# TensorE's order written by hand in the SSD stage of a two-layer hybrid decoder trunk

## The chip, the cores and the metric

The program runs on one core of a Trainium2 chip. It is measured in microseconds of device time; the time of a kernel is the median of its runs.

## The reference

A prompt of 256 tokens and 8 sample sequences of 4 tokens each pass through the same two layers. The kernel holds all 288 tokens as the columns of one tile (NT = 288). A layer is a half-step FFN, a mixer with two branches, and a second half-step FFN:

```python
x = x + 0.5 * swiglu(rmsnorm(x, norm_ffn1[l]), w_ffn1_gu[l], w_ffn1_down[l])
m, g_s, s_s, c_s = mixer(rmsnorm(x, norm_mix[l]), ...)
x = x + m
x = x + 0.5 * swiglu(rmsnorm(x, norm_ffn2[l]), w_ffn2_gu[l], w_ffn2_down[l])
```

```python
q, k, v, g, a_lr, z, xbc, dt_raw, gate_a, gate_b = jnp.split(u @ w_in, offs, axis=-1)
...
o_gla = rmsnorm(o_gla, gla_norm)
o_gla = o_gla * silu(g)
xbc_c = silu(causal_dwconv(xbc, conv0, conv_w, conv_b))
xs, Bm, Cm = jnp.split(xbc_c, ...)
y, ssm_new = ssd_chunked(xs, dt, A, Bm, Cm, ssm0)
y = rmsnorm((y + d_skip * xs) * silu(z), ssm_norm)
m = sigmoid(gate_a) * (o_gla @ w_proj_gla) + sigmoid(gate_b) * (y @ w_proj_ssm)
return m @ w_out, gla_new, ssm_new, conv_new
```

GLA is a chunked linear attention with a matrix state for each of 8 sequences and 4 heads. SSD is a chunked scan over 32 heads of width 64, in 4 groups that share B and C, with a 64 x 128 state for each of 8 sequences and 32 heads. The new states of both are outputs. Everything is float32.

## The kernel before, in words

**Projections.** Almost all of the work is the product of a weight matrix with the 288 token columns. A float32 weight block of 128 output columns is loaded as 128 x 8 x 128 and split by `split` into a high part (ACT, a copy, tile wh) and the rest (DVE or POOL, a subtraction, tile wl); the activations are split in the same way (xh, xl). A block is then 24 matmuls of 288 columns into one PSUM tile psg, of which there are three. `mm3` writes them: for each of 8 slices wh with xh and wh with xl (L177 and L178), then wl with xh for all 8 (L180). In this document a projection is one such matmul of 288 columns. `blocks` (L182) makes a sequence of such blocks.

**Small products.** Everything else on TensorE goes to PSUM tiles pst, of which there are four: transposes (`tr`, L142) and the products of the scans.

**Who sets the order.** The kernel is written in a tile framework whose scheduler orders each engine's instructions, TensorE's among them. The code says which blocks are interleaved with which stage: `gla` and `ssd` are generators, and at each `yield n` the loop `run` (L510) lets `F` emit n fill blocks. `F` (L503) is the sequence of the z, g, gate_gla and gate_ssm blocks with the GLA's output projection between them. Each `yield` of `F` is one whole block or, in `gated` and `project` (L550 to L564), a block and a projection.

**The end of GLA (L830 to L847).** The sums of squares of four heads are made by TensorE with a matrix of ones, two products for each head (L835, 8 in all), in four row groups of one PSUM tile. ACT takes the root (L837), DVE the reciprocal (L838), ACT and DVE split it in two rows of rp (L840, L841). At `yield 1` (L842) a fill block is emitted. Then four products of 2 rows (L845) spread rp over 128 partitions, and DVE scales o8 with it.

**The SSD stage (`ssd`).** It works on 16 pairs of heads, j = 0 to 15; an iteration is one j. Two j make a state pair hg, four j make a group g.
- `stage_bc(g)` projects the group's B and C blocks and runs the causal convolution (`conv`, L854) on each: ACT copies the block to a buffer, POOL adds the old columns, ACT and DVE sum four taps and apply SiLU. `stage_group(g)` transposes B, makes the scores C x B (three products, L933 to L935) and masks them. `stage_mask(g)` makes bm, eight copies of B with all but one sequence's rows zero (128 rows x 8 x 128, L952), in one buffer.
- `stage_x(j)` projects the block of xs and convolves it; `stage_m(j)` transposes it (three `tr`), scales it twice on DVE (xg at L1025, xd at L1028) and makes the decay mask m.
- `stage_load(j)` loads the states of 2 heads and 8 sequences into two tiles st (L962) of eight buffers, so those of four j. `stage_h(hg, i)` transposes four 128 x 128 states (L142) and copies them to sh; `stage_h2(hg, 3)` reads all of the pair's states with C (8 products, L985) and scales the result to yos (L990).
- `stage_y(j)` decays the states (8 POOL instructions of 128 columns, L1046), makes the scan's four products of m and xg (L1052, L1054), the sample's product (L1055) and the prompt's new state (L1057, L1058). DVE, POOL and ACT make y, the gated yf, its split yh and yr, and its squares. Then two products of 512 columns (L1076) make the state update, xpk x bm over 128 rows; DVE adds it to the states (L1078), and SP's queue stores them (L1080).

In iteration j come the load for j+3, transposes of the next pair, the projection of xs for j+2, state reads, `stage_m(j+1)`, a fill block, a transpose, `stage_y(j)` and one more fill block (two at every fourth j). After the last iteration `proj` (L519) emits the fill blocks that are left and the SSD's output projection.

## Time and profile before

| | us |
|---|---|
| median of 3 runs | 1853.45 |
| the runs | 1853.57, 1853.45, 1852.42 |
| profiled execution, its own time | 1856.72 |
| profiled execution, span of the trace | 1854.1 |

| engine | busy, share of the span | instructions |
|---|---|---|
| PE (matmul) | 98% | 13712 |
| DVE | 67% | 2074 |
| ACT | 56% | 1866 |
| POOL | 20% | 553 |

The trace is of one profiled execution; the time of that execution is a little longer than its span, by what lies around it. PE is TensorE's matmuls, PEld its weight loads, which lie beside them. The ends of matmuls are modelled, so the idle time of PE is known less well than the starts. PEclk is the clock that TensorE was granted, 1.00 being 2.4 GHz and 0.50 being 1.2 GHz; over the whole span it was 0.997. The first layer's SSD stage lies at about 375 to 645 us of the span, the second layer's at about 1290 to 1560 us.

### The profile page before, as it was taken

To read this page: it belongs to the slowest core of one execution; us is meant where nothing else is said; L and a number is where in the kernel's file an instruction comes from. 1 tells how busy PE (TensorE), PEld (TensorE's weight loads), DVE (VectorE), ACT (ScalarE), POOL (GpSimd) and SP (SyncE) were. 2 spreads that over 40 slices of the span, in tenths; PEclk is the share of its full clock that TensorE was granted. 3 is DMA by queue.
4 is the path that set the end of the run, shared out by engine and by line. 5 is a ranking of instruction groups with operands and counts; after the bars stand their busy time and mean duration, and the time that the engine had idled before them with its cause. 6 is when DMAs were issued, how large, how long until landed. Compare 5 with 4: busy or idle time off the path is not lost. (4 is left out here: it accounts for less than half of the span.)

```text
span 1854.1 us, 35076 instructions
## 1 busy us (share of the span) xinstructions
PE 1815.0 (98%) x13712; PEld 1745.5 (94%) x13712; DVE 1237.8 (67%) x2074; ACT 1038.3 (56%) x1866; POOL 377.6 (20%) x553
## 2 busy tenths in 40 slices
PE   8999999999999999999999999999999999999997
PEld 8999999888989899999999999998899888999997
DVE  6555577688877767555565556776887777665554
ACT  6444466567766646444454445665776675454443
POOL 1000000057667500000000000000777663000000
PEclk9999999999999999999999999999999999999999
DMA  7555654876778565555555555568587775655552
GB/s 214 166 164 158 165 153 127 262 193 180 212 194 223 166 169 173 165 166 162 172 167 161 161 164 158 144 183 251 153 225 199 199 206 151 172 165 165 162 162 89
DMA packets 613114, 325.43 MB, mean 176 GB/s; under 512 B 17090, under 2 KB 607986, under 8 KB 612948
## 3 DMA queue, kind: packets, MB, share of 16 engines
q1 hardware_dynamic: 612900, 323.07, 61.0%
q8 instruction: 107, 1.75, 0.4%
q14 instruction: 59, 0.48, 0.1%
q10 hardware_dynamic: 48, 0.13, 0.0%
HBM read 292.93 MB, written 30.22 MB: 174 GB/s over the span
## 5 line engine op out<-in xcount | busy, mean ns | idle before, releaser
L158 ACT ACTIVATE wh<-wr 128x1024 fp32r<-128x1024 f32 (+1 forms) x498 | 517.7, 1042 | 479.2 <-PE psg L178 384.6
L177 PE MATMUL psg<-xh,wh 128*128 128x288 f32 x2704 | 740.0, 300 | 2.8 <-ACT t L867 2.2
L178 PE MATMUL psg<-xl,wh 128*128 128x288 f32 x2704 | 734.5, 297 | 0.1
L164 DVE TENSOR_TENSOR wl<-wr,wh 128x1024 fp32r<-128x1024 f32 (+1 forms) x496 | 596.9, 1206 | 151.7 <-ACT wh L158 147.0
L177 PEld LDWEIGHTS psg<-xh,wh 128*128 128x128 f32 x2704 | 508.0, 188 | 9.7 <-issue 6.2
L178 PEld LDWEIGHTS psg<-xl,wh 128*128 128x128 f32 x2704 | 508.1, 188 | 3.3 <-issue 0.9
L180 PE MATMUL psg<-xh,wl 128*128 128x288 f32 x2704 | 416.1, 296 | 0.0
L180 PEld LDWEIGHTS psg<-xh,wl 128*128 128x128 f32 x2704 | 378.3, 188 | 2.0 <-issue 0.9
L1046 POOL TENSOR_SCALAR st<-st,decs 128x128 f32<-128x128 f32 x256 | 228.7, 907 | 18.7 <-PE pst L142 18.6
L177 PE MATMUL psg<-hh,wh 128*128 128x288 f32 x704 | 189.8, 296 | 0.0
L178 PE MATMUL psg<-hl,wh 128*128 128x288 f32 x704 | 189.5, 295 | 0.0
L372 POOL MEMSET cbuf<- 128x3 f32 x4 | 0.3, 108 | 654.4 <-DVE t L324 654.4
L178 PEld LDWEIGHTS psg<-hl,wh 128*128 128x128 f32 x704 | 132.7, 188 | 0.0
L177 PEld LDWEIGHTS psg<-hh,wh 128*128 128x128 f32 x704 | 132.2, 188 | 0.1
L304 DVE TENSOR_TENSOR t<-t,psg 128x288 f32<-128x288 f32 x88 | 40.0, 454 | 135.2 <-ACT wh L158 123.1
L180 PE MATMUL psg<-hh,wl 128*128 128x288 f32 x704 | 109.2, 295 | 0.0
L301 DVE TENSOR_TENSOR t<-psg,rr 128x288 f32<-128x288 f32 x88 | 40.3, 457 | 90.5 <-PE psg L180 90.5
L180 PEld LDWEIGHTS psg<-hh,wl 128*128 128x128 f32 x704 | 99.0, 188 | 0.0
L865 DVE SCALAR_TENSOR_TENSOR cacc<-cbuf,cw,cacc 128x312 f32<-128x312 f32 x144 | 78.1, 542 | 11.1 <-ACT cacc L863 10.7
L177 PE MATMUL psg<-yh,wh 128*128 128x288 f32 x256 | 70.2, 300 | 0.0
L178 PE MATMUL psg<-yb,wh 128*128 128x288 f32 x256 | 69.4, 296 | 0.7 <-DVE yb L1070 0.7
L177 PE MATMUL psg<-oh,wh 128*128 128x288 f32 x256 | 69.7, 299 | 0.0
(315 smaller groups left out, 2287.9 us busy)
## 6 DMA issues: line engine op xcount, KB each, us to landing
wr<-in_w_ffn_gu_dram SPq DMA_DIRECT2D x176, 512.0 KB
wr<-in_w_in_dram SPq DMA_DIRECT2D x160, 512.0 KB
wr<-in_w_ffn_down_dram SPq DMA_DIRECT2D x64, 448.0 KB
wr<-in_w_ffn_down_dram SPq DMA_DIRECT2D x32, 512.0 KB
st<-in_state_ssm_dram SPq DMA_DIRECT2D x64, 256.0 KB
out_dram<-st SPq DMA_DIRECT2D x64, 256.0 KB
wr<-in_w_proj_ssm_dram SPq DMA_DIRECT2D x32, 512.0 KB
gst<-in_state_gla_dram SPq DMA_DIRECT2D x32, 256.0 KB
```

The lines of the kernel that those rows point to most:

```text
L158: A.activation(out=h, in_=raw, func=AF.Copy)
L164: V.tensor_tensor(out=lo, in0=raw, in1=h, op=ALU.subtract)
L177: T.matmul(out, lhsT=h[:, k], rhs=xh[k], start=start and k == 0, stop=False)
L178: T.matmul(out, lhsT=h[:, k], rhs=xl[k], start=False, stop=False)
L180: T.matmul(out, lhsT=lo[:, k], rhs=xh[k], start=False, stop=stop and k == n - 1)
L301: V.tensor_tensor(out=t, in0=pg, in1=r, op=ALU.mult)
L304: V.tensor_tensor(out=h, in0=t, in1=pu, op=ALU.mult)
L372: G.memset(cbufs[i][:, 0:3], 0.0)
L865: V.scalar_tensor_tensor(out=acc, in0=buf[:, i:i + NCV], scalar=w[i], in1=acc, op0=ALU.mult, op1=ALU.add)
L1046: G.tensor_scalar(out=sts[hf][:, r], in0=sts[hf][:, r], scalar1=decs[:, n:n + 1], scalar2=None, op0=ALU.mult)
```

## The change

TensorE's order in the SSD stage is no longer the scheduler's. A flag `in_order` is set from the start of the stage's loop to its end, and while it is set every matmul and transpose is passed to `keep_in_program_order`, so that TensorE runs them as they are written. Other engines are still ordered by the scheduler.

- A block of 24 projections is now emitted in thirds of 8 (`mm3s`, `thirds`): a generator stops after the slices 0 to 3 and 4 to 7 of wh, and after the eight of wl. `D(n)` deals n thirds, first from `jobs` (the queue of convolution blocks that the stage has asked for), then from `F`. Calls of `D` stand between the small products of an iteration.
- The group products of the next group come at j%4 == 2, with a third between the transposes and the scores. The masks are made with them.
- `bm` has four copies instead of eight (seq4 for seq8), in two buffers instead of one. The first half of the rows of xpk holds sequences 0 to 3, the second half 4 to 7, so that the update is two products of 512 columns over 64 rows each (rows 0 to 63 and 64 to 127). The two state tiles of a j now hold sequences 0 to 3 and 4 to 7 instead of even and odd ones, and `stage_h` and `state_view` follow.
- The 16 decays of a state pair are emitted together right behind the pair's last transposes (`stage_decay`), instead of 8 in each `stage_y`.
- At j == 13 the first halves of the output projection's blocks 0 and 1 are put into `jobs` (`begin`); each holds its psg tile until `proj` completes it.

The core of the diff:

```diff
     def tr(out, in_, k=128):
-        T.transpose(out, in_, ident[0:k, 0:k])
+        ins = T.transpose(out, in_, ident[0:k, 0:k])
+        if in_order[0]:
+            tc.keep_in_program_order(ins)
...
-    def mm3(out, h, lo, xh, xl, start, stop):
+    in_order = [False]
+
+    def mm(*a, **k):
+        ins = T.matmul(*a, **k)
+        return tc.keep_in_program_order(ins) if in_order[0] else ins
+
+    def mm3s(out, h, lo, xh, xl, start, stop):
+
         n = h.shape[1]
         for k in range(n):
-            T.matmul(out, lhsT=h[:, k], rhs=xh[k], start=start and k == 0, stop=False)
-            T.matmul(out, lhsT=h[:, k], rhs=xl[k], start=False, stop=False)
+            mm(out, lhsT=h[:, k], rhs=xh[k], start=start and k == 0, stop=False)
+            mm(out, lhsT=h[:, k], rhs=xl[k], start=False, stop=False)
+            if k % 4 == 3:
+                yield False
         for k in range(n):
-            T.matmul(out, lhsT=lo[:, k], rhs=xh[k], start=False, stop=stop and k == n - 1)
+            mm(out, lhsT=lo[:, k], rhs=xh[k], start=False, stop=stop and k == n - 1)
+
+    def mm3(*a):
+        for _ in mm3s(*a):
+            pass
...
+    def thirds(src, x, nblk):
+
+        for b in range(nblk):
+            h, lo = weights(src[:, b * 128:(b + 1) * 128])
+            p = psg()
+            yield from mm3s(p, h, lo, x[0], x[1], True, True)
+            yield b, p
...
             def run(gen):
                 for n in gen:
                     for _ in range(n or 0):
-                        next(F, None)
+                        while next(F, True) is False:
...
+            begun = {}
+
+            def begin(j, yh):
+
+                begun[j] = psg()
+                yield from projects(begun[j], w_proj_ssm[l], j, [yh[:, k] for k in range(16)], yr, 0, 8)
+                yield False
...
-                    late.append((j, project(w_proj_ssm[l], j, [yh[:, k] for k in range(16)], yr)))
+                    p = begun[j] if j in begun else psg()
+                    for _ in projects(p, w_proj_ssm[l], j, [yh[:, k] for k in range(16)], yr, 8 * (j in begun)):
+                        pass
...
+            jobs = []
+
+            def D(n):
+
+                for _ in range(n):
+                    while jobs:
+                        if next(jobs[0], None) is not None:
+                            break
+                        jobs.pop(0)
+                    else:
+                        next(F, None)
...
             def stage_mask(g):
+
                 bpk = R["g", g][2]
-                bm = sp_.tile([128, NS, 128], F32R, name="bm", tag="bm", bufs=1)
-                for s in range(NS):
-                    A.activation(out=bm[:, 4 * (s % 2) + s // 2], in_=bpk, func=AF.Copy, scale=C["seq8"][:, s:s + 1])
+                bm = sp_.tile([128, 4, 128], F32R, name="bm", tag="bm", bufs=2)
+                for s in range(4):
+                    A.activation(out=bm[:, s], in_=bpk, func=AF.Copy, scale=C["seq4"][:, s:s + 1])
                 R["bm", g] = bm
 
             def state_view(t, j, hf):
-                return t[l, hf:NS:2, 2 * j:2 * j + 2].rearrange("s h p d -> (h p) s d")
+                return t[l, 4 * hf:4 * hf + 4, 2 * j:2 * j + 2].rearrange("s h p d -> (h p) s d")
...
-                    st = R["st", 2 * hg + a % 2][i // 2]
-                    tr(p[:, a * 128:(a + 1) * 128], st[:, 2 * (i % 2) + a // 2])
+                    st = R["st", 2 * hg + a % 2][i % 2]
+                    tr(p[:, a * 128:(a + 1) * 128], st[:, 2 * (a // 2) + i // 2])
...
+            def stage_decay(hg):
+
+                for j in (2 * hg, 2 * hg + 1):
+                    for hf in range(2):
+                        st = R["st", j][hf]
+                        for r in range(4):
+                            n = 8 * j + 4 * hf + r
+                            G.tensor_scalar(out=st[:, r], in0=st[:, r], scalar1=decs[:, n:n + 1], scalar2=None,
+                                            op0=ALU.mult)
...
-                for hf in range(2):
-                    for r in range(4):
-                        n = 8 * j + 2 * r + hf
-                        G.tensor_scalar(out=sts[hf][:, r], in0=sts[hf][:, r], scalar1=decs[:, n:n + 1], scalar2=None,
-                                        op0=ALU.mult)
...
+                mm(y[:, sp], lhsT=yo2, rhs=ms[:, j % 4], start=True, stop=True)
+                D(1)
...
+                D(1)
+                pu = [pst(), pst()]
                 for hf in range(2):
-                    p = pst()
-                    T.matmul(p, lhsT=xpk, rhs=bm[:, 4 * hf:4 * hf + 4].rearrange("p s d -> p (s d)"),
-                             start=True, stop=True)
+                    rows = slice(64 * hf, 64 * hf + 64)
+                    mm(pu[hf], lhsT=xpk[rows], rhs=bm[rows].rearrange("p s d -> p (s d)"), start=True, stop=True)
+                for hf in range(2):
...
+            in_order[0] = True
             for j in range(3):
                 stage_load(j)
-            yield 1
-            stage_pack(0)
-            stage_x(0)
+            jobs.append(stage_bc(0))
+            jobs.append(stage_x(0))
+            D(6)
+            stage_h(0, 0)
+            D(3)
+            stage_h(0, 1)
+            D(3)
             stage_group(0)
-            yield 1
-            stage_x(1)
-            stage_mask(0)
-            stage_h(0, 0)
-            yield 1
-            stage_h(0, 1)
-            stage_h2(0, 0)
+            jobs.append(stage_x(1))
+            D(3)
+            stage_h(0, 2)
+            D(1)
             stage_m(0)
-            stage_h(0, 2)
-            stage_h2(0, 1)
-            yield 1
+            D(2)
             stage_h(0, 3)
+            stage_decay(0)
+            D(2)
             for j in range(16):
                 g, hg = j // 4, j // 2
                 odd, nx = j % 2, hg < 7
                 if j + 3 < 16:
                     stage_load(j + 3)
-                if odd and nx:
+                if j + 2 < 16:
+                    jobs.append(stage_x(j + 2))
+                D(3)
+                if not odd:
+                    stage_h2(hg, 3)
+                    D(1)
+                elif nx:
                     stage_h(hg + 1, 1)
-                if j + 2 < 16:
-                    stage_x(j + 2)
-                if not odd:
-                    stage_h2(hg, 2)
-                    stage_h2(hg, 3)
-                elif nx:
-                    stage_h2(hg + 1, 0)
-                if j == 0:
-                    stage_bc(1)
-                    stage_pack(1)
                 if j + 1 < 16:
                     stage_m(j + 1)
-                yield 1
+                D(1)
                 if nx:
                     stage_h(hg + 1, 2 if odd else 0)
-                    if odd:
-                        stage_h2(hg + 1, 1)
-                if j == 1 or j in (4, 8):
+                if j % 4 == 0 and g < 3:
+                    jobs.append(stage_bc(g + 1))
+                D(2)
+                if j % 4 == 2 and g < 3:
                     stage_group(g + 1)
+                    D(1)
+                if j == 13:
+                    jobs.extend((begin(0, yh), begin(1, yh)))
                 stage_y(j)
-                if odd and nx:
-                    stage_h(hg + 1, 3)
-                if j % 4 == 3 and g < 3:
-                    stage_mask(g + 1)
-                    if g < 2:
-                        stage_bc(g + 2)
-                        stage_pack(g + 2)
-                yield (2 if j % 4 == 3 else 1)
+                D(1)
+                if odd:
+                    if nx:
+                        stage_h(hg + 1, 3)
+                        stage_decay(hg + 1)
+                    D(1)
+            in_order[0] = False
```

What follows is the order of the instructions in the two programs. A row is an operation with the tile it writes, the tiles it reads, its shape, and how many follow one another. psg<-xh,wh and psg<-xl,wh and psg<-xh,wl of 128x288 are projections (L177, L178 and L180 before; L180 in the change, where the helper `mm` writes all of them).

First TensorE at the end of GLA in the first layer. L835 (L888 in the change) is the last sum of squares, L845 (L898) the products with rp. Before:

```order
L177 MATMUL psg<-xh,wh 128x288
L178 MATMUL psg<-xl,wh 128x288
L835 MATMUL pst<-t_4202,call 32x288
L180 MATMUL psg<-xh,wl 128x288 x8
...
L180 MATMUL psg<-xh,wl 128x288 x8
L177 MATMUL psg<-xh,wh 128x288
L845 MATMUL pst<-rp,ones_r 128x288 x4
L178 MATMUL psg<-xl,wh 128x288
```

The change:

```order
L180 MATMUL psg<-xh,wh 128x288
L180 MATMUL psg<-xl,wh 128x288
L888 MATMUL pst<-t_4202,call 32x288
L180 MATMUL psg<-xh,wl 128x288 x8
L898 MATMUL pst<-rp,ones_r 128x288 x4
L180 MATMUL psg<-xh,wh 128x288
L180 MATMUL psg<-xl,wh 128x288
```

Before, 57 projections stand between the last sum and the products with rp; in the change 8 do, and the products come ahead of the blocks that they stood behind. The second layer reads alike.

Second TensorE in an iteration of the SSD stage, around the scan's products. Before (L142 transposes states, L1052 to L1058 are the scan's products, L1076 is the update):

```order
L180 MATMUL psg<-xh,wl 128x288 x8
L142 MATMUL pst<-call,st 128x128 x4
L1052 MATMUL pst<-m,xg 64x256
L1054 MATMUL pst<-m,xg 64x128
L1052 MATMUL pst<-m,xg 64x256
L1054 MATMUL pst<-m,xg 64x128
L1055 MATMUL pst<-msm,yos 128x32
L1057 MATMUL pst<-bt,xd 128x128
L1058 MATMUL pst<-bt,xd 128x128
L1076 MATMUL pst<-bm,xpk 128x512 x2
```

The change:

```order
L180 MATMUL pst<-m,xg 64x256
L180 MATMUL pst<-m,xg 64x128
L180 MATMUL pst<-m,xg 64x256
L180 MATMUL pst<-m,xg 64x128
L180 MATMUL pst<-msm,yos 128x32
L180 MATMUL psg<-xh,wl 128x288 x8
L180 MATMUL pst<-bt,xd 128x128 x2
...
L180 MATMUL pst<-bm,xpk 128x512 x2
```

Before, transposes, scan products and update stand in one group with no projection between; in the change a third of a block stands between the sample's product and the prompt's state, and another (8 projections, left out above) ahead of the update.

Third SP's queue at j = 1, where the states of one j are stored (L1080, L1162 in the change), the prompt's new state too (so), and those of another j loaded (L962, L1033); acb is a broadcast row of decays, wr a weight block. Before:

```order
L1083 DMA out_dram<-so 128x2x128
L1080 DMA out_dram<-st 128x4x128
L1002 DMA acb<-acd 128x512
L1080 DMA out_dram<-st 128x4x128
L171 DMA wr<-in_w_in_dram 128x8x128
L962 DMA st<-in_state_ssm_dram 128x4x128 x2
```

The change:

```order
L1165 DMA out_dram<-so 128x2x128
L1162 DMA out_dram<-st 128x4x128 x2
L1033 DMA st<-in_state_ssm_dram 128x4x128 x2
L174 DMA wr<-in_w_in_dram 128x8x128 x4
L1084 DMA acb<-acd 128x512
```

The two loads now stand right behind the two stores; before, a load of acb and one of a weight block stood between.

## Rows read from the trace of the kernel before

**Rows 1.** The page's first part: engine, busy us, share of the span, instructions.
```profile
PE 1815.0 (98%) x13712; PEld 1745.5 (94%) x13712; DVE 1237.8 (67%) x2074; ACT 1038.3 (56%) x1866; POOL 377.6 (20%) x553
```
**Rows 2.** Stretches: us, length, PE, PEld, DVE, ACT, POOL busy (count), PEclk, DMA, GB/s.
```profile
100.00:200.00 100.00, 100.00 (x752) 100.00 (x752) 54.22 (x76) 44.76 (x59) 0.00 (x0) 1.00 0.56 162
375.00:645.00 270.00, 259.57 (x1993) 239.49 (x1993) 214.50 (x387) 186.13 (x431) 182.60 (x260) 0.99 0.71 196
400.00:500.00 100.00, 97.29 (x751) 89.81 (x751) 89.12 (x164) 71.53 (x167) 72.36 (x102) 1.00 0.72 198
1290.00:1560.00 270.00, 259.25 (x1997) 239.01 (x1997) 213.21 (x383) 185.26 (x430) 182.97 (x260) 1.00 0.70 195
```
**Rows 3.** The same view for L177, L178, L180 alone: PE, PEld, PEclk, DMA, GB/s.
```profile
375.00:645.00 270.00, 127.99 (x465) 87.75 (x465) 0.99 0.71 196
375.00:645.00 270.00, 125.56 (x464) 87.52 (x465) 0.99 0.71 196
375.00:645.00 270.00, 72.44 (x468) 66.00 (x467) 0.99 0.71 196
```
**Rows 4.** PE's timeline: start, us, engine, line, operation, tiles, shapes, count.
```profile
420.44 0.60 PE L142 MATMUL pst<-call,st 128*128 128x128 f32 x4
...
421.01 0.29 PE L178 MATMUL psg<-xl,wh 128*128 128x288 f32 x1
```
**Rows 5.** PE's timeline, an iteration's small products from first to the projection behind.
```profile
414.66 0.60 PE L142 MATMUL pst<-call,st 128*128 128x128 f32 x4
...
417.35 0.29 PE L178 MATMUL psg<-xl,wh 128*128 128x288 f32 x1
```
**Rows 6.** PE's waits, 375 to 645: tile, line, releaser, us, times, longest.
```profile
PE pst L933 <- DVE bcf L869: 2.2, 1, 2.2
PE pst L142 <- ACT sh L974: 1.5, 2, 0.9
```
**Rows 7.** Stretches around the first group's wait, columns of rows 2.
```profile
384.70:387.90 3.20, 1.02 (x8) 0.92 (x7) 2.04 (x7) 3.17 (x11) 0.75 (x4) 1.00 1.19 290
387.90:391.30 3.40, 3.40 (x16) 3.38 (x16) 1.85 (x5) 2.33 (x9) 0.96 (x2) 0.50 0.29 74
```
**Rows 8.** Timeline of all engines at the end of GLA, first layer.
```profile
363.51 0.67 PE L835 MATMUL pst<-t,call 128*32 128x288 f32 x2
...
364.12 1.36 PE L180 MATMUL psg<-xh,wl 128*128 128x288 f32 x8
...
366.04 0.50 ACT L837 ACTIVATE t<-pst,eps 128x288 f32<-128x288 f32 x1
...
366.71 1.95 DVE L838 RECIPROCAL t<-t 128x288 f32<-128x288 f32 x1
...
369.99 0.44 ACT L840 ACTIVATE rp<-t 128x288 fp32r<-128x288 f32 x1
...
371.27 0.51 DVE L841 SCALAR_TENSOR_TENSOR rp<-rp,call,t 128x288 fp32r<-128x288 f32 x1
...
371.67 0.29 PE L177 MATMUL psg<-xh,wh 128*128 128x288 f32 x1
...
371.89 0.40 PE L845 MATMUL pst<-rp,ones_r 2*128 2x288 f32 x4
...
372.46 0.29 PE L177 MATMUL psg<-xh,wh 128*128 128x288 f32 x1
```
**Rows 9.** Line L845 in both layers: count, ns shortest, median, longest, first and last.
```profile
L845 PE MATMUL pst<-rp,ones_r x8: 392/392/393, 371.9 to 1284.7; 2*128 2x288 f32 x8
```
**Rows 10.** Line L1046, the decays of the states, in both layers.
```profile
L1046 POOL TENSOR_SCALAR st<-st,decs x256: 596/605/2781, 390.3 to 1541.9; 128x128 f32<-128x128 f32 x128
```
**Rows 11.** Timelines of DVE, SP's queue (SPq) and PE, 434 to 445.
```profile
434.35 0.67 DVE L1078 TENSOR_TENSOR st<-st,pst 128x512 f32<-128x512 f32 x1
438.62 2.77 SPq L962 DMA_DIRECT2D st<-in_state_ssm_dram  x2
444.61 0.60 PE L142 MATMUL pst<-call,st 128*128 128x128 f32 x4
```

More of the change, by code (lines that the diff above doesn't have):

```diff
@@ L470, in fill_z @@
             def fill_z():
-                for j, (pg,) in blocks([W[:, O_Z:O_Z + 2048]], X, 16):
+                for it in thirds(W[:, O_Z:O_Z + 2048], X, 16):
+                    if not it:
+                        yield False
+                        continue
+                    j, pg = it
                     yf[j] = yblk(F32)
@@ L994, in stage_x @@
             def stage_x(j):
-                _, (pg,) = next(xs_blocks)
-                xs, buf = conv(pg, j, "xs", 3)
+                while not (it := next(xs_blocks)):
+                    yield False
+                xs, buf = conv(it[1], j, "xs", 3)
                 conv_last(j, buf)
@@ L1003, in stage_x @@
                 R["x", j] = xs, x4, acb
+                yield False
             def stage_m(j):
```

87 lines of the change are left out of this document (54 added, 33 removed).

## The prediction

> **What bounds the kernel now.** I read the page's first part, then the table of stretches, then PE's rows in the SSD stage. TensorE is busy 98% of the span [rows 1], and where only projections run it is full: 752 matmuls in 100 us, 0.133 us each [rows 2]. No order shortens such a stretch. The SSD stage is different. It lies at about 375 to 645 us in the first layer and 1290 to 1560 us in the second, and there PE idles 270 - 259.57 = 10.4 us and 270 - 259.25 = 10.8 us [rows 2]. DVE, the next engine, works 214.5 of those 270 us, and is at 89% only from 400 to 500 us [rows 2].
>
> Ends of matmuls are modelled, so idle time understates what is lost. I therefore count products. From 375 to 645 us there are 465 + 464 + 468 = 1397 projections [rows 3], 186 us at 0.133. The other 84 us hold the small products. Four state transposes cost 421.01 - 420.44 - 0.133 = 0.44 us: from the first of them to the second projection behind, less one projection [rows 4]. Transposes, scan products and state update together take 417.35 - 414.66 - 0.133 = 2.56 us in an iteration where nothing waits [rows 5]. Sixteen of these (41), sixteen more groups of transposes (7), sixteen groups of three xs transposes at three quarters of 0.44 (5), and, as an estimate from the rates of these, 1.2 us for each of 8 state reads and 4 sets of group products (14) make 67 us. So 84 - 67 = 17 us of the first layer are waits, of which the records show 10.4. The largest are the first group's scores, 2.2 us behind the conv, then transposes of states behind copies of sh [rows 6]. They include the clock: PE worked 1.02 us from 384.7 to 387.9, and from 387.9 to 391.3 its granted clock was 0.50 (1.2 GHz) [rows 7]; half of 3.4 us is 1.7 us.
>
> **The change, part by part.** There are 11,712 projections before and after, and as many small products; work is moved, and PE's order in the SSD stage is pinned.
>
> *Thirds between small products.* A seam costs nothing: four transposes between projections take 0.11 us each [rows 4]. What goes is the waiting inside long groups: scan products, then the update that needs the masks, then transposes that need a PSUM buffer. Now 8 projections (1.06 us) stand at each seam, and the masks are made two iterations before use. At stake are 17 us, and 15.3 in the second layer, whose clock stays at 1.00 [rows 2], in all 32. I keep 3 as counting error: -29 us.
>
> *Waits that stay or are new in the stage.* Per layer: the first B and C convs are still chained, with 24 projections and two groups of transposes ahead of their products, 1 us. The two half-projections begun early hold two of three psg buffers, so four gate blocks at the end wait for the tanh of the block before, 1.5 us as an estimate (four times the 0.4 us of a 288-column ACTIVATE such as the copy to rp [rows 8]). The last scan product has 8 or 9 projections behind it before its yh is needed, 1 us. Queues of DVE and POOL, 1.5 us. Together 5, for both layers +10 us; bounds 0 and the present 32.
>
> *The GLA norm's product.* Of this cost I am surest. Before, 57 projections stand between the last sum of squares (L835) and the product with rp (L845); now 8. PE runs matmuls in order, so it waits for the chain. The last sum starts at 363.51 and its 8 projections at 364.12, so PE would be free at 364.12 + 8 x 0.133 + 0.1 = 365.3 [rows 8]. The square root ends at 366.54 and the reciprocal at 368.66; then come the copy, 0.44, and the correction, 0.51 [rows 8]. ACT and DVE now run both ahead of the weight split, so with hand-overs of some 0.1 us the product starts at about 369.9. PE idles 4.6 us, where before L845 started 0.22 us behind the projection ahead of it [rows 8]. A shorter idle has brought the lower clock [rows 7], so I add 1.7 us. The second layer has the same rows [rows 9]: +12.6 us; bounds 2 x 4.6 without the clock, 2 x 8 if it falls twice.
>
> *The update on half the rows.* Two 512-column products over 128 rows become two over 64 rows that can run beside each other. No row shows such a pair. The nearest is L845, four products of 288 columns in four row groups, which start together [rows 8]. They cost 371.89 - 371.67 - 0.133 = 0.09 us on the way in and 372.46 - 371.89 - 0.133 = 0.44 behind, 0.52 together: as much as four in turn, so 0.39 us goes into the changeover. A pair would take one pass of 512/288 x 0.133 = 0.24 plus up to 0.39, 0.63 at most; two in turn take 0.47. The state read's column groups start in the same manner, so I take two thirds of that loss, 0.10 us x 32 = +3 us; bounds -7.5 (a pass saved in each of 32 pairs, no changeover) and +5. The Trainium skill's "TensorEngine Tiling" (Theoretical Speedup) gives up to 2x where a dimension is 64 or less, by which the sum would be 10.5 us lower; its Key Properties say that changing the tiling mode drains the engine, and L845's row agrees with that.
>
> *Masks and decay.* Half of the mask copies leave ACT, which is off the path, and the decays on POOL start a step earlier, in runs of up to 5. POOL works 183 of 270 us [rows 2]. A conv's buffer copy behind such a run is some 3 us late (5 at 0.6 [rows 10]); an iteration of about 14 us (10 thirds and 3.7 us of small products) lies between the conv and its use, and if that cover went, xs would hold PE up. Cost 0.
>
> **Sum.** -29 + 10 + 12.6 + 3 = -3.4 us. The profiled execution took 1856.72 and would take 1853.3; it stands 3.3 us above the median of the runs, 1853.45. My forecast for the median is **1850 us**.
>
> **Rivals.**
> *More is won: 1833 us, 0.26.* All 32 us of waits go, 3 us per layer stay, the clock does not fall in the norm's wait, and half of the pairs' 7.5 us is real: -32 + 6 + 9.2 - 3.7 = -20.5. For it: undisturbed groups cost just their products [rows 4, 5]. Against: the changeover at L845, and an idle of 2 us that brought the lower clock [rows 7, 8].
> *DVE sets the pace: 1857 us, 0.15.* With PE quicker, the first third of the stage asks DVE for more than 89% [rows 2], and products wait for its scaled xs and its PSUM reads; 8.5 us per layer stay instead of 5, +7. Against: 79% over the whole stage.
> *Slower: 1864 us, 0.22.* The reload of the states. At iteration j the tile for j+3 takes the buffers of j-1, so update, store, load and transposes are one chain. In the trace the update starts at 434.35, the loads are issued from 438.62, and the transposes start at 444.61 [rows 11], 10.3 us after the update. In the new order there are 56 projections (7.4 us), four transposes, a state read and three transposes (1.9 us) between the update's products and those transposes, 9.3 us, and PE cannot step past them. There are 6 such places per layer. At 1.25 us each, 12 x 1.25 = 15 less 1 us of the queues' share gives 1864; at 0.3 us the gain is gone, and from 0.6 us the kernel is slower. Against: SP now issues both loads right behind both stores, without the acb and weight loads between.
>
> **How the numbers follow.** 0.2% (3.7 us) is about what a measurement of this kernel can tell from no change: faster is under 1849.7, slower over 1857.2. The forecast's own case has 0.37 and spans 1844 to 1856; half of it lies under 1849.7. Faster: 0.26 + 0.19 = 0.45, and a little of the others where one term comes out low, 0.47. Slower: 0.22 and under half of the DVE case, 0.28. The rest, 0.25, is no change. The range of 8 in 10 runs from the middle of the best case to that of the worst, 1831 to 1864.
>
> **What would show it.** Right: in both layers one PE wait of 4 to 5 us before the product with rp, released by DVE, with a granted clock of 0.5 behind it; PE idle in the rest of the stage near 5 us per layer instead of 10; the two update products starting together, the next projection some 0.3 us or more behind. Wrong: no such wait; transposes of st that wait for a DMA at every even iteration; DVE over 95% in the first third; or idle as long as before, spread over many small waits.

## The result and the profile after

The change makes the kernel slower. Its median of 4 runs is 1866.53 us (1865.19 to 1869.62) against 1853.51 us for the kernel before, a ratio of 1.0065 with a 95% interval of 1.0051 to 1.0078. That is 12 to 13 us more, where the forecast was 1850 us. The profiled execution took 1865.72 us, its span is 1863.9 us, and 9.8 us longer than the span before.

The page's first part of the changed kernel, beside [rows 1]:

```profile
PE 1823.1 (98%) x13712; PEld 1748.9 (94%) x13712; DVE 1248.1 (67%) x2074; ACT 1030.3 (55%) x1834; POOL 383.3 (21%) x553
```

The two SSD stretches, columns as in [rows 2]:

```profile
375.00:645.00 270.00, 262.29 (x2006) 241.00 (x2005) 218.04 (x383) 181.61 (x412) 184.61 (x260) 0.99 0.69 191
1290.00:1560.00 270.00, 262.69 (x2004) 241.45 (x2004) 218.93 (x384) 181.35 (x413) 183.82 (x260) 0.99 0.70 193
```

PE looks busier than before (262.3 of 270 us against 259.6) and idles less, yet the kernel is slower. Two things hide in that: the stretches no longer hold the same part of the program, and a matmul at half clock counts as busy for longer (0.45 us at 560.87, 0.29 at full clock). DVE's 218 us in the first layer are 3.5 more than before; it still idles 52 of the 270 us, so it isn't the bound.

PE's waits over the whole span (tile, line, releaser; us in total, times, longest) have three large entries in the two stages, where [rows 6] had many small ones:

```profile
PE pst L898 <- DVE rp L894: 8.5, 2, 4.3
PE pst L143 <- DMA st<-in_state_ssm_dram: 6.2, 4, 3.2
PE psg L180 <- ACT t L606: 6.1, 4, 2.3
```

**The norm's product**, in the timeline of all engines, first layer; it answers to [rows 8]:

```profile
363.21 1.36 PE L180 MATMUL psg<-xh,wl 128*128 128x288 f32 x8
...
365.80 1.94 DVE L891 RECIPROCAL t<-t 128x288 f32<-128x288 f32 x1
...
368.26 0.52 DVE L894 SCALAR_TENSOR_TENSOR rp<-rp,call,t 128x288 fp32r<-128x288 f32 x1 [0.20 <-ACT rp L893]
368.83 0.40 PE L898 MATMUL pst<-rp,ones_r 2*128 2x288 f32 x4 [4.26 <-DVE rp L894]
```

PE waits 4.26 us for rp. Behind this wait its granted clock falls, as it does behind most of the other long ones; the stretches (columns of rows 2) behind the norm, the reload and the tanh in the first layer, and behind the norm in the second:

```profile
369.50:372.90 3.40, 3.40 (x16) 3.40 (x15) 2.51 (x4) 0.00 (x0) 0.00 (x0) 0.50 0.63 181
...
437.80:441.20 3.40, 3.40 (x18) 3.38 (x16) 2.59 (x6) 2.17 (x5) 2.82 (x4) 0.50 0.35 101
560.70:564.10 3.40, 3.40 (x16) 3.40 (x16) 2.34 (x3) 1.22 (x2) 3.40 (x5) 0.50 0.64 192
1287.70:1294.50 6.80, 6.65 (x29) 6.40 (x30) 2.84 (x5) 1.06 (x1) 0.00 (x0) 0.50 0.66 189
```

At 0.50 (1.2 GHz) projections start 0.24 us apart instead of 0.133, so a stretch of 3.4 us loses about 1.5. The changed kernel has three of them in the first layer's stage (369.5, 437.8 and 560.7 us) and in the second one of 6.8 us (1287.7) and one of 3.4 (1478.9), 20.5 us in all and 9 us lost; the kernel before had a single one of 3.4 us in the two stages together.

**The reload of the states**, answering to [rows 11] (DVE's, SP's and PE's timelines):

```profile
428.99 1.27 DVE L1160 TENSOR_TENSOR st<-st,pst 128x512 f32<-128x512 f32 x2
429.69 1.01 SPq L1162 DMA_DIRECT2D out_dram<-st  x2
433.85 1.08 SPq L1033 DMA_DIRECT2D st<-in_state_ssm_dram  x2
433.33 0.27 PE L143 MATMUL pst<-call,st 128*128 128x128 f32 x1
436.86 0.33 PE L143 MATMUL pst<-call,st 128*128 128x128 f32 x1 [3.25 <-DMA st<-in_state_ssm_dram]
```

PE makes one transpose and waits 3.25 us for the tile whose load was issued at 433.85. The update's products ran at 423.34, for 0.50 us; DVE added them only at 428.99, 5.1 us after their end.

**The gate's tanh** (PE's and ACT's timelines):

```profile
485.05 1.30 PE L180 MATMUL psg<-xh,wl 128*128 128x288 f32 x8
...
494.45 0.46 ACT L920 ACTIVATE t<-cacc 128x312 f32<-128x312 f32 x1 [0.43 <-DVE cacc L918]
494.82 0.39 ACT L606 ACTIVATE t<-psg 128x288 f32<-128x288 f32 x1
...
495.26 0.40 PE L180 MATMUL psg<-xh,wh 128*128 128x288 f32 x1 [0.88 <-ACT t L606]
```

The gate block's last third is done at 486.3, its tanh (L606) comes only at 494.82, behind a convolution's tanh (L920), and the next xs block waits for the tile that it frees. TensorE's order shows why (the blocks named by the program's order, the starts of their thirds, us): the gate block had two thirds dealt, then three convolution blocks of 24 projections jumped ahead, and only then came its last third:

```
gate              468.57, 469.99
xs                472.01, then the other two, the last from 475.37
B                 476.87, 478.55, 479.71
C                 480.77, then the other two, the last from 483.56
gate, last third  485.05
```

**An account of the stretch.** The change touches what lies between the last sum of squares and the SSD's last output projection. I split it in each layer at the first state update: the hand-over from GLA, and the rest. Waits are its length less the work: per layer 1807 projections at 0.1326 us, and the small products at the lengths that their groups have where nothing waits, 7.6 us in the hand-over and 61.8 behind (64.4 with half-row pairs). These lengths are estimates from the traces. The waits include what the clock takes. Us, both layers together:

| kernel | ratio to before, 95% interval | hand-over waits | waits behind | length |
|---|---|---|---|---|
| before | 1 | 10.6 | 24.5 | 653.2 |
| the change | 1.0065 (1.0051 to 1.0078) | 15.7 | 24.5 | 663.3 |
| e1 pinned later | 1.0080 (1.0064 to 1.0095) | 17.9 | 25.0 | 666.1 |
| e2 decays back | 1.0062 (1.0044 to 1.0079) | 15.5 | 27.8 | 666.4 |
| e3 all rows | 1.0060 (1.0039 to 1.0081) | 14.9 | 26.6 | 659.4 |
| e4 transposes later | 1.0026 (1.0017 to 1.0036) | 15.3 | 17.8 | 656.1 |
| e5 blocks closed | 0.9971 (0.9960 to 0.9982) | 14.1 | 8.2 | 645.4 |
| e6 12 thirds first | 1.0091 (1.0075 to 1.0108) | 21.8 | 28.2 | 673.2 |
| e7 e4 + e5 + e6 + rows | 0.9947 (0.9935 to 0.9959) | 15.1 | 9.5 | 642.6 |
| e8 not pinned | 1.0081 (1.0065 to 1.0097) | 20.9 | 22.8 | 666.7 |
| e9 e4 + e5 + rows | 0.9942 (0.9928 to 0.9957) | 14.0 | 9.3 | 641.3 |
| e10 e9 + a block | 0.9965 (0.9952 to 0.9979) | 14.4 | 13.9 | 646.3 |
| e11 a block | 1.0043 (1.0027 to 1.0059) | 13.9 | 20.4 | 657.4 |
| e12 e4 + e5 | 0.9962 (0.9948 to 0.9976) | 14.0 | 6.0 | 643.1 |
| e13 e9, no rp | 0.9889 (0.9873 to 0.9906) | 2.4 | 9.5 | 628.8 |
| e14 e9, none begun | 0.9937 (0.9921 to 0.9953) | 13.6 | 8.6 | 640.2 |

Behind the hand-over the change waits as long as before, 24.5 us. To that come 5.1 us of hand-over and 5.1 us of half-row pairs, in all the 10.1 us by which the stretch is longer. The ratios come from medians on the chips that ran them, the other columns from one profiled execution each, so differences of a us or two between rows are not shown by them.

### The profile page after: what moved, and what is told of

Read it like the earlier page. It is cut to its first block, busy times and chain, and to the rows that moved or that the text cites. A ratio compares the mean times of both kernels' runs of the same rounds, so it can differ in the third digit from the quotient of the medians.

```text
span 1863.9 us, 35058 instructions
## 1 busy us (share of the span) xinstructions
PE 1823.1 (98%) x13712; PEld 1748.9 (94%) x13712; DVE 1248.1 (67%) x2074; ACT 1030.3 (55%) x1834; POOL 383.3 (21%) x553
## 4 chain that ended last, share of the span: by engine, by line
PE 52%; DMA 2%; DVE 2%; ACT 2%; POOL 1%; issue 1%; SPq 0%; DVEq 0%; ACTq 0%; POOLq 0%
PE psg L180 48%; PE pst L180 2%; DMA out_dram<-st 1%; PE pst L143 1%; DMA st<-in_state_ssm_dram 1%; POOL st L1055 1%; ACT wh L161 0%; DVE wl L167 0%; DVE cacc L918 0%; PE pst L847 0%; SPq L1033 0%; DMA wr<-in_w_in_dram 0%; DVE st L1160 0%; PE gyo L838 0%; PE yo L180 0%
## 5 line engine op out<-in xcount | busy, mean ns | idle before, releaser
L161 ACT ACTIVATE wh<-wr 128x1024 fp32r<-128x1024 f32 (+1 forms) x498 | 518.0, 1041 | 485.3 <-PE psg L180 396.4
L180 PE MATMUL psg<-xh,wh 128*128 128x288 f32 x2704 | 752.2, 303 | 6.5 <-ACT t L606 6.1
L180 PE MATMUL psg<-xl,wh 128*128 128x288 f32 x2704 | 741.1, 299 | 0.1
L167 DVE TENSOR_TENSOR wl<-wr,wh 128x1024 fp32r<-128x1024 f32 (+1 forms) x496 | 598.3, 1207 | 179.2 <-ACT wh L161 154.9
L180 PEld LDWEIGHTS psg<-xh,wh 128*128 128x128 f32 x2704 | 512.4, 190 | 21.7 <-issue 9.7
L180 PEld LDWEIGHTS psg<-xl,wh 128*128 128x128 f32 x2704 | 513.1, 190 | 2.5 <-issue 0.9
L180 PE MATMUL psg<-xh,wl 128*128 128x288 f32 x2704 | 421.4, 298 | 0.0
L180 PEld LDWEIGHTS psg<-xh,wl 128*128 128x128 f32 x2704 | 378.7, 189 | 4.9 <-issue 4.7
L180 PE MATMUL psg<-hh,wh 128*128 128x288 f32 x704 | 189.8, 296 | 0.0
L180 PE MATMUL psg<-hl,wh 128*128 128x288 f32 x704 | 189.5, 295 | 0.0
L180 PEld LDWEIGHTS psg<-hl,wh 128*128 128x128 f32 x704 | 132.7, 188 | 0.0
L180 PEld LDWEIGHTS psg<-hh,wh 128*128 128x128 f32 x704 | 132.2, 188 | 0.1
L180 PE MATMUL psg<-hh,wl 128*128 128x288 f32 x704 | 109.2, 295 | 0.0
L180 PEld LDWEIGHTS psg<-hh,wl 128*128 128x128 f32 x704 | 99.0, 188 | 0.0
L918 DVE SCALAR_TENSOR_TENSOR cacc<-cbuf,cw,cacc 128x312 f32<-128x312 f32 x144 | 83.4, 579 | 9.8 <-ACT cacc L916 8.8
L180 PE MATMUL psg<-yh,wh 128*128 128x288 f32 x256 | 70.8, 303 | 1.7 <-ACT wh L161 1.2
L180 PE MATMUL psg<-oh,wh 128*128 128x288 f32 x256 | 72.1, 306 | 0.0
L180 PE MATMUL psg<-ob,wh 128*128 128x288 f32 x256 | 69.5, 296 | 0.0
```

The lines of the kernel that those rows point to most:

```text
L161: A.activation(out=h, in_=raw, func=AF.Copy)
L167: V.tensor_tensor(out=lo, in0=raw, in1=h, op=ALU.subtract)
L180: ins = T.matmul(*a, **k)
L918: V.scalar_tensor_tensor(out=acc, in0=buf[:, i:i + NCV], scalar=w[i], in1=acc, op0=ALU.mult, op1=ALU.add)
```

## The experiments

**e1: the order pinned later.** The flag is set behind the first six thirds.

```diff
-            in_order[0] = True
             for j in range(3):
...
             D(6)
+            in_order[0] = True
             stage_h(0, 0)
```

> The order is pinned only from the first state transposes on, so that the first B and C blocks may again stand ahead of the products with rp. Theory (the norm's wait and the clock behind it are one of four costs): in the changed kernel TensorE idles 4.3 us ahead of these products in each layer, and its granted clock is 0.5 for 3.4 us behind it in the first layer and 6.8 in the second; at 0.24 instead of 0.133 us for a projection these lose 1.5 and 3.1 us. All go: 8.6 + 4.6 = 13 us less than the changed kernel, about 1853. Rival A (the clock falls as often, only elsewhere): 8.6 us less, 1858. Rival B (TensorE runs ahead and another engine, DVE above all, sets the pace, so the wait turns up behind): under 3 us less, 1864 or more.

No wait for rp is left, and the kernel is no faster: ratio 1.0080. PE's waits:

```profile
PE pst L143 <- DMA st<-in_state_ssm_dram: 16.9, 7, 4.5
```

and SP's queue behind rp:

```profile
374.55 3.83 SPq L1033 DMA_DIRECT2D st<-in_state_ssm_dram  x6
```

The first state loads are issued only behind rp's products (373.98), which release SP's queue: the state tiles use GLA's memory. The first transposes now come 4.9 us after these products and wait 4.5 us, with 10.2 us at half clock around them. This is rival B, except that PE waits for a load and not for DVE.

**e2: the decays back in stage_y.**

```diff
-            stage_decay(0)
...
                 y = pst()
+                for hf in range(2):
+                    for r in range(4):
...
```

> The decays of the states go back into stage_y, 8 for each pair of heads, and everything else stays as changed. Theory (the run of decays on POOL holds the convolution's buffer copy, ACT's next instruction waits for that copy, and the gate block's tanh stands behind it on ACT): TensorE's waits for that tanh, 0.9 + 2.1 us in the first layer and 0.8 + 2.3 in the second, go, and with them two stretches at half clock of 3.4 us (1.5 us each): 9 us less than the changed kernel, about 1857.5. Rival (the tanh is late because a gate block dealt in thirds holds its PSUM and temporary tiles longer, wherever the decays stand): the waits stay within 1 us and the time within 2 us of the changed kernel.

PE's waits:

```profile
PE pst L143 <- DMA st<-in_state_ssm_dram: 9.5, 4, 3.4
...
PE psg L180 <- ACT t L606: 6.1, 4, 2.3
```

My theory falls: the tanh is waited for exactly as long. The decays' early place is no loss; without it the reload is later (9.5 us instead of 6.2).

**e3: the update over all rows.**

```diff
-                    rows = slice(64 * hf, 64 * hf + 64)
-                    mm(pu[hf], lhsT=xpk[rows], rhs=bm[rows]...
+                    mm(pu[hf], lhsT=xpk, rhs=bm...
```

> Both update products run over all 128 rows with the same four masks, instead of 64 rows each; each state then also gets the update of the sequence four further, so the sample states are not the reference's, and no instruction is added or taken away. Theory (the two row halves do not run beside each other to any gain, and the change of tile costs time): the pair falls from 0.627 to 0.47 us, 32 x 0.157 = 5.0 us less than the changed kernel. Rival (0.627 is what two passes cost anyway with a third on each side): within 1 us of the changed kernel.

PE's timeline of the same update in the change,

```profile
422.12 1.30 PE L180 MATMUL psg<-xh,wl 128*128 128x288 f32 x8
423.34 0.50 PE L180 MATMUL pst<-bm,xpk 64*128 64x512 f32 x2
423.78 0.40 PE L180 MATMUL psg<-xh,wh 128*128 128x288 f32 x1
424.02 0.30 PE L180 MATMUL psg<-xl,wh 128*128 128x288 f32 x1
424.15 0.30 PE L180 MATMUL psg<-xh,wh 128*128 128x288 f32 x1
```

and in e3:

```profile
424.08 1.30 PE L180 MATMUL psg<-xh,wl 128*128 128x288 f32 x8
425.21 0.63 PE L180 MATMUL pst<-bm,xpk 128*128 128x512 f32 x2
425.68 0.29 PE L180 MATMUL psg<-xh,wh 128*128 128x288 f32 x1
425.81 0.29 PE L180 MATMUL psg<-xl,wh 128*128 128x288 f32 x1
425.94 0.29 PE L180 MATMUL psg<-xh,wh 128*128 128x288 f32 x1
```

From the eight projections ahead of the pair to the third behind it are 2.03 us with half rows and 1.86 with all: 0.17 us a pair. The two halves do run beside each other (both within 0.50 us), but the pair starts 1.22 us after the eight instead of 1.13, and the second projection behind it comes 0.24 us after the first instead of 0.13. The 30 pairs that stand between projections are alike: less the projections around it, a pair costs 0.62 to 0.63 us in the change's trace and 0.46 to 0.47 in e3's. The stretch is 3.9 us shorter; the rest of the 5 us comes back as longer waits. The ratio alone (1.0060) can't tell e3 from the change.

**e4: the transposes of even iterations two thirds later.**

```diff
-                if nx:
-                    stage_h(hg + 1, 2 if odd else 0)
+                if nx and odd:
+                    stage_h(hg + 1, 2)
...
                 D(2)
+                if nx and not odd:
+                    stage_h(hg + 1, 0)
```

> In even iterations the first transposes of the next pair's states come two thirds of a block (2.1 us) later. Theory (the reload of a state tile ends too late for them at the first place where buffers come round): the waits for the load, 3.25 us in the first layer and 2.4 in the second, shrink to 1.1 and 0.3, and the stretch at half clock behind the first goes (1.5 us): 5.8 us less than the changed kernel, about 1860.5. Rival (DVE is late there with the update itself, and the next product waits for DVE instead): under 2 us less.

As expected: 7.2 us less in the stretch, one wait of 0.93 us for a load left, a new one of 1.3 us for yos in the second layer, and no half clock behind either. The second layer's last tanh has no half clock behind it in this trace, so some 1.5 of the 7.2 us need not be the edit's. The rest shows the reload as a cost of its own.

**e5: an open block is closed first.**

```diff
-                    while jobs:
+                    while jobs and not part[0]:
...
                     else:
-                        next(F, None)
+                        part[0] = next(F, None) is False
```

> One edit to the changed kernel: a fill block of which a third has been dealt is finished before the convolution blocks that ask for their turn. Theory (the first and third gate blocks are left open while two or three convolution blocks jump the queue; the gate's tanh then stands on ACT behind the last of their convolutions, and the next block needs the PSUM tile that the tanh frees): TensorE's four waits for that tanh, 6.1 us in all in the changed kernel, fall under 1 us, and the two stretches at half clock behind them (1.5 us each) go: 9 us less than the changed kernel, a ratio to the kernel before of about 1.0015. Rival (ACT is late there whatever the blocks' order, and the wait goes over to a convolution block, which now comes up to two thirds later): within 2 us of the changed kernel, ratio 1.0055 to 1.0075.

The largest effect of all edits to the changed kernel, and more than expected: 17.9 us less in the stretch, faster than the kernel before. No wait for L606 is in the list any more, and what is left of the three large ones is

```profile
PE pst L898 <- DVE rp L894: 8.5, 2, 4.3
...
PE pst L143 <- DMA st<-in_state_ssm_dram: 3.5, 2, 1.8
```

Of the 16.3 us by which the waits behind the hand-over fall, 6.1 are the tanh, 2.7 the reload, and 4.6 three stretches at half clock (437.8, 560.7 and 1478.9), which no longer occur. The remaining 3 us I can't assign to single rows.

**e6: twelve thirds ahead of the first transposes.**

```diff
             jobs.append(stage_x(0))
-            D(6)
+            jobs.append(stage_x(1))
+            D(12)
+            in_order[0] = True
             stage_h(0, 0)
...
```

> One edit to the changed kernel: 12 thirds instead of 6 stand ahead of the first state transposes (the second xs block comes early), and the order is pinned only behind them; as many thirds fewer stand between the first group's small products. Theory (at the hand-over from GLA two things are late, the norm's rp and, as soon as TensorE doesn't wait for that, the first state loads, which can't be issued before GLA's buffers are free; 104 projections between the last sum of squares and the first transposes, where there were 56, cover both): the waits for rp (2 x 4.3) and those for the first loads (5.5 us in each layer where the pin alone came later) both go, and the 10.2 us at half clock behind rp (4.6 us): 13 us less than the changed kernel, ratio 0.9995. Rival A (the thirds missing between the first group's products bring as much waiting there): ratio 1.003 or more. Rival B (the loads still come late): a wait for the state load of over 2 us, ratio over 1.004.

This is rival A, and worse than it said: the waits for rp and the first loads are gone, but the first group's products wait for their convolution, in PE's waits from 370 to 420 us:

```profile
PE pst L180 <- DVE bcf L922: 2.7, 1, 2.7
PE pst L143 <- DVE xs L922: 2.0, 1, 2.0
```

with 10.2 us at half clock between 388 and 402. Projections were taken from where they covered these.

**e7: four edits together** (e4, e5, e6, and eight masks over all rows).

```diff
+                    mm(pu[hf], lhsT=xpk, rhs=bm[:, 4 * hf:4 * hf + 4]...
...
+                if j % 4 == 3 and g < 3:
+                    stage_mask(g + 1)
```

> Four edits to the changed kernel together: 12 thirds ahead of the first transposes, open fill blocks finished first, the transposes of even iterations two thirds later, and the update over all 128 rows with eight masks again (made behind each fourth iteration, in one buffer). Theory (the four costs are apart, and what is left of the order by hand is its gain): against the changed kernel -13, -9, -7 (as measured) and -4, 33 us in all, so some 20 us less than the kernel before, ratio 0.989. Rival (DVE and ACT set the pace once TensorE's waits are gone, and the waits return in other places): half of that at most, ratio 0.997 or more.

Half of the expected gain: 0.9947, and by the account 15.1 us of hand-over are left. The e6 edit gives nothing here either; e9, which leaves it out, is as fast.

**e8: not pinned.**

```diff
-            in_order[0] = True
+            in_order[0] = False
```

> The changed kernel with the order left to the scheduler throughout: thirds, masks, decays and all else stay. The scheduler's order moves the products with rp behind 57 projections again, and splits the first groups of transposes, and leaves most of the rest as written. Theory (the norm's wait is the pin's doing, the waits for the reload and for the gate's tanh are the dealing's): the wait for rp goes, a wait for the first state load of 2 to 3 us comes in its place (81 projections are between, 3.3 us more than where 56 left 5.5 us), the others stay: 4 to 8 us less than the changed kernel, ratio 1.002 to 1.0045. Rival (pinning as such costs, since TensorE can't step past any late product): all waits go, ratio under 0.997.

Neither the theory nor the rival: there is no wait for rp, but state loads and packed samples are waited for in the hand-over (20.9 us), the tanh as before. Without the pin the kernel is no faster, so pinning as such isn't what costs.

**e9: three edits** (e7 without e6).

> The changed kernel with three edits: open fill blocks finished first (ratio 0.9971 to the kernel before by itself), the transposes of even iterations two thirds later, and the update over 128 rows with eight masks. Theory (each is a cost by itself): the waits for the reload that were left at 1.65 and 1.82 us go, 3.5 us, and the pairs give 32 x 0.17 = 5.5; 9 us less than with the first edit alone, ratio 0.992. Rival (as much waiting comes back at ACT, which makes twice the masks in one buffer, and at DVE): ratio 0.9955 or more.

Between the theory (0.992) and the rival (0.9955): 0.9942, 1844.05 against 1853.89 us; e7 and e14 are as fast within their intervals, and of the kernels that compute everything none is faster. The waits for the reload did go but for one of 0.3 us; against e5 the stretch is only 4.1 us shorter instead of 9, since other waits grew (e12). The two stretches, columns as in [rows 2]:

```profile
375.00:645.00 270.00, 268.00 (x2088) 251.25 (x2087) 223.82 (x389) 188.99 (x438) 181.05 (x262) 1.00 0.73 199
1290.00:1560.00 270.00, 267.47 (x2086) 250.61 (x2084) 225.39 (x390) 187.24 (x430) 177.53 (x255) 1.00 0.71 194
```

PE idles 2.0 and 2.5 us, and does 2088 matmuls where the change did 2006.

**e10 and e11: one fill block more ahead of the norm's product**, on e9 and on the change.

```diff
-            yield 1
+            yield 2
             for hd in range(4):
                 p = pst()
```

> The three edits, and one fill block (24 projections, 3.2 us) more ahead of the products with rp; three thirds fewer stand in the last iteration. Theory (the norm's wait is worth what the changed kernel's trace shows): the wait of 4.3 us falls to 1.1 in both layers and the clock doesn't fall behind it (1.5 and 3.1 us): 11 us less than with the three edits alone, ratio 0.986. Rival A (the clock falls all the same): 6.4 us less, 0.9885. Rival B (the first group's conv, or the last iteration, waits instead): under 3 us less, 0.9905 or more.

> One edit to the changed kernel: one fill block more ahead of the products with rp, three thirds fewer in the last iteration. Theory (the norm's wait and the clock behind it, 13 us of the changed kernel's time, are the hand-over's cost and nothing else waits there): 2 x 3.2 + 4.6 = 11 us less than the changed kernel, ratio 1.0006. Rival (the hand-over is bound by the chain of loads and convolutions behind GLA, so the wait turns up behind, as it did where the order was pinned later): under 3 us less, ratio 1.005 or more.

24 projections cover 3.2 us, but the wait shrinks only from 4.26 to 3.13. ACT's and DVE's timelines of e11 show why:

```profile
366.89 0.50 ACT L890 ACTIVATE t<-pst,eps 128x288 f32<-128x288 f32 x1
...
369.52 0.41 ACT L501 ACTIVATE yb<-psg 128x288 f32<-128x288 f32 x1 [0.41 <-PE psg L180]
369.82 1.05 ACT L161 ACTIVATE wh<-wr 128x1024 fp32r<-128x1024 f32 x1
370.77 0.43 ACT L893 ACTIVATE rp<-t 128x288 fp32r<-128x288 f32 x1
370.90 1.22 DVE L167 TENSOR_TENSOR wl<-wr,wh 128x1024 fp32r<-128x1024 f32 x1 [0.49 <-ACT wh L161]
372.05 0.51 DVE L894 SCALAR_TENSOR_TENSOR rp<-rp,call,t 128x288 fp32r<-128x288 f32 x1
```

The added block's tanh (L501) and a weight split (L161) stand ahead of the copy to rp (L893), which starts 3.9 us after the root instead of 2.65 (365.13 and 367.78 us in the change). DVE's part of that split (L167) then stands ahead of the correction, which starts 0.85 us after the copy ends instead of 0.04. Together that is nearly all of the 2.1 us that the block fails to cover. On e9 waits for the tanh come back as well (3.3 us), and e10 is slower than e9 where 11 us were expected of it; on the change the edit gives 5.9 us in the stretch, ratio 1.0043, between theory and rival.

**e12: the three edits without the rows.**

> The three edits without the third: the update keeps its 64 rows and four masks. Theory (a pair of half-row products takes 0.63 us where two whole ones take 0.456, and nothing else hangs on it): 5 us more than with the three edits, ratio 0.9945 beside 0.992. Rival (the eight masks on ACT cost as much as the pair saves): the same as with the three edits within 1.5 us.

0.9962 beside 0.9942 (1847.83 and 1844.05 us on one chip; the intervals overlap), between the theory and the rival. The pairs' 5.1 us are there (0.62 to 0.63 us each, in e9 0.46 to 0.47). In e9 the waits are 3.3 us longer, so its stretch gains 1.8. Part of that is that state reads wait for sh (0.32 and 0.59 us), whose copy stands on ACT right behind four of the eight mask copies; e12 has no such wait. That the masks cause the rest isn't shown.

**e13: the norm's end left out.**

```diff
-            ro = t1()
-            A.activation(out=ro, in_=p[:, 0:NT], func=AF.Sqrt, ...
...
             yield 1
-            for hd in range(4):
...
```

> The best kernel so far (three edits) without the end of the GLA norm: root, reciprocal, rp, its four products and the scaling of o8 are left out, so the GLA branch is not normalized. Theory (the norm's product costs what its rows show, 2 x 4.26 us of waiting and 4.6 us of half clock): 13 us less than with the three edits, ratio about 0.987, and no wait over 1 us between the last sum of squares and the first state update. Rival (behind it stand the first state loads and the first convolutions, which are late by as much): a wait for a state load or for bcf of over 2 us in its place, under 5 us less, ratio 0.9915 or more.

The theory holds: 12.5 us less in the stretch, of which 1.0 are the eight products left out, and the hand-over's waits fall from 14.0 to 2.4 us. In the hand-over one wait of 1.0 us for a packed sample is left, and no half clock. So the chain of the norm bounds the hand-over.

**e14: no output projection begun early** (e9 without the two calls of `begin` at j == 13).

> The three edits without the two half-projections that are begun early, so that no PSUM tile is held over the last gate blocks; 48 projections fewer stand between the last scan products. Theory (the held tiles cost the waits of 0.75 and 0.4 us ahead of the output projection in each layer): these go, 2.3 us less, ratio 0.993. Rival (without these projections the last two iterations' small products wait for DVE and ACT): 3 us more or worse, ratio 0.9955 or more.

The same as e9 by the ratios, so neither the theory's gain nor the rival's loss is shown. The waits ahead of the output projection go; a wait of 2.1 us for a reload, with half clock behind it, comes in the second layer.

## Why the prediction was wrong

*What bounds the kernel* held: some 32 us of waits were estimated in both layers, 35.1 by the account.

*Thirds between small products, -29.* The small waits did go. With two faults of the dealing mended (e12), 6.0 us are left behind the hand-over of 24.5. A seam is indeed free: the 36 groups of four transposes that stand alone between projections in e12 cost 0.43 to 0.44 us each, as in [rows 4].

*Waits that stay or are new, 5 us a layer.* **This step failed.** Behind the hand-over 24.5 us came instead of some 8 (four of the five us a layer) and the 3 kept as counting error: 13.5 us too few, as much as the sum is off (-3.4 forecast, +10.1 measured in the stretch); the other terms' errors, 1.1 in the hand-over, 2.1 in the pairs and 3.1 in the waits before, cancel. I put the gate's waits at the two tiles that `begin` holds, 1.5 us a layer; the waits there measured 0.75 + 0.4 us a layer in e9, were released by a weight split and by yh instead of a tanh, and go in e14. I didn't see that `D` serves `jobs` ahead of a fill block already open, which holds its PSUM tile and puts its tanh behind convolutions on ACT. Finishing the open block first takes 16.3 us of these waits away (e5), some 3 of them not assigned to rows. The rule stood in the diff, and its effect in TensorE's order. With the reload's transposes moved as well, 6.0 us are left (e12), fewer than the 11 forecast.

*The GLA norm's product, +12.6.* Right: 4.26 us of waiting where 4.6 were forecast, the lower clock behind both, 11.6 us of waits gone when it is taken away (e13). Covering it did not pay in full: e1, e6 and e8 brought other waits in its place, and e11 got back 5.9 us of the 11 expected.

*The update on half the rows, +3.* Right in sign, at its bound: 0.63 us a pair, the 0.63 that I gave as the most, 5.1 us in all. The Trainium skill ("TensorEngine Tiling (Array Packing)", Theoretical Speedup) gives up to 2x where a dimension is 64 or less. The traces don't bear that out for such a pair alone: it took 0.63 us where two whole products in turn take 0.46.

*Masks and decay, 0.* For the decays right as to the time (e2: 1.0062 beside 1.0065), and their early place helps the reload. What half the masks are worth stays open; e12 and e9 hint that it is more than nothing.

*The rivals.* The reload (0.22, 1864 us) came, but with weight at one place a layer, not six: 3.25 and 2.4 us, and 0.3 and 0.2 at a second. It was worth 7.2 us (e4) where I priced 15, so that its 1864 lies so near the measured time is luck. DVE never was the bound: from 400 to 500 us it worked 85.2 us in the change, 89.1 before [rows 2].

So the time lies above the range because the scattered waits, none over 2.2 us, gave way to as much in few long ones, and the norm's wait and the pairs came on top. The lower clock came with the long ones: 9 us lost, where I had counted it behind the norm alone.

## What to carry to other kernels

Where an order is dealt by hand from several queues, finish a block that has begun before another queue gets its turn: an open block holds its PSUM tile, and its evacuation falls behind what was emitted meanwhile, here on ACT. Fewer waits are not less waiting: price each long one with the half clock that may follow it. Before covering a wait with more work, look whether that work's own ACT and DVE instructions stand ahead of the chain that is waited for.

## What was not expected of the hardware

The same idle doesn't always bring the lower clock. In the changed kernel a wait of 2.4 us at 1354.3 us left it at 1.00, and one of 2.1 us at 557.9 was followed by 3.4 us at 0.50. A wait of 0.83 us in the second layer's GLA stands in both traces (1176 us before, 1180 after); only in the change's did half clock follow (1181.9 to 1185.3).

The pace of projections differs between executions at a full granted clock. In the same stretch of FFN, 740 to 900 us, which no edit touches, the trace of before has

```profile
740.00:900.00 160.00, 160.00 (x1217) 159.82 (x1216) 89.12 (x124) 73.63 (x99) 0.00 (x0) 1.00 0.56 166
```

and that of e1

```profile
740.00:900.00 160.00, 160.00 (x1183) 159.82 (x1183) 86.51 (x121) 72.19 (x97) 0.00 (x0) 1.00 0.55 161
```

0.1315 and 0.1352 us for each, both at 1.00; the slower pace lengthened that FFN by 4.8 us. There are two values in the first layer and none between: from the SSD's last output projection to the FFN's last matmul, 1781 matmuls, eleven of the sixteen traces take 235.7 us and five (e1, e2, e3, e13, e14) 240.4. In the second layer all sixteen take 239.4 to 239.5. What decides stays open. So the verdicts of single edits are read from the stretch that they touch as well as from the medians.
